# The entry of the odd layer, written out by hand over four engines: x's root before ctx's share, keys and values tile by tile

## The chip, the cores and the metric

The kernel runs on one core of one Trainium2 chip. The metric is the device time of one execution in microseconds; times inside an execution are microseconds from the start of its profiled span. PE is the matmul engine (TensorE), PEld its weight loads, DVE VectorE, ACT ScalarE, POOL GpSimd, and SP the engine whose queue issues most loads.

## The reference

Two layers of a transformer over 512 tokens `x` and 256 context tokens `ctx`, width 1024. Each layer modulates a normalised input, mixes tokens, and adds a gated feed-forward part (FFN). Around the change stand the end of layer 0's FFN and the entry of layer 1 (the odd one):

```python
y = xf * lax.rsqrt(jnp.mean(xf * xf, axis=-1, keepdims=True) + EPS)      # rmsnorm, then * g
modulate(x, g, shift, scale) = rmsnorm(x, g) * (1 + scale) + shift
q, k, v = jnp.split(h @ w_qkv, [C_Q_WIDTH, C_Q_WIDTH + C_KV_WIDTH], axis=-1)   # 1024, 256, 256 columns
q, k = apply_rope(q, cos, sin), apply_rope(k, cos, sin)
kc, vc = jnp.split(hc @ w_qkv[:, C_Q_WIDTH:], 2, axis=-1)                # ctx gives keys and values, no queries
```

The odd layer then attends in blocks of 128 queries, each to a band of three blocks of x's keys and to all of ctx's keys, with a sink in the softmax. ctx itself is not needed after this layer's keys and values.

## The kernel before

Everything lies transposed: eight tiles of 128 features (`m` or `k`, 0 to 7) by 512 columns of x or 256 of ctx. Each float32 factor is split in a high part (a cast on ACT) and a low part (the difference, on POOL or DVE), and `mm3` (L102) multiplies with three matmuls, high by high, high by low and low by high (L106, L107, L108): one product. `unit` (L73) loads 128x512 of a weight over SP into one of a few raw buffers and splits it (L81 ACT, L84 POOL) into a slot of the ring; a load waits until POOL is done with its raw buffer, a split until PE is done with its slot.

PSUM has eight banks: `bank` takes the next of three, `fill` a single one, `single` the next of four, or in their place `wide` the next of two pairs. A tile that is asked for again waits until the last reader of its old contents is done. SBUF pools are stacked from the left and from the right; a tile of a pool opened in the place of a released one waits for the readers of what lay there.

A planner orders the instructions of each engine by its own model of time. Where an instruction is issued under `tc.issue_after(other)`, it stays behind the other one on its engine. `run` (L876) uses that: whatever is issued with `run("PE", ...)` (or "DVE", "ACT", "POOL") forms a chain in the order of the code.

`ffn(0)` works on 22 hidden blocks, in a list of units written as letters (L1084): digits are products of the first FFN matrix, `s` and `t` parts of the second. `s2_part` (L1049) multiplies two hidden blocks (or one) for feature tile m into a bank, and `residual` (L774) adds the result, times a gate, to x or ctx in SBUF. The last two blocks (20 and 21) are the remainder: six of the eight tiles m take block 20 ahead, for x and for ctx (the units `efghij`, L1255), while block 21 is finished; then a loop (L1272) runs the rest, x's eight tiles first, then ctx's, and behind each tile squares it (`square`, L780) and adds the squares. Three or four tiles of squares are added up, the other four are handed to PE as they are.

`modulated` (L793) then forms the root for x, and for ctx: PE sums the squares over partitions against a matrix of ones (L156, L161), DVE takes the inverse root with three Newton steps in tiny instructions (L135 to L139), and writes it on the diagonal of a 128x128 block for each 128 columns (L173), and PE spreads that to all partitions with one matmul against ones (L183). Each tile k is then modulated in three steps: DVE scales it by gain and root (L199), ACT adds the shift and rounds to the high part (L200), DVE makes the low part (L201). This, and all of `odd`, is left to the planner.

`odd` (L1298) opens its PSUM pools and its ring (three raw buffers, four slots), loads the rotation tables, the mask and the sink (L1308 to L1314), and projects keys: `project_k` (L1321) runs eight products of 512 columns for x and eight of 256 for ctx, rotates x's keys (`rope`, L248, DVE and POOL), and stacks high and low parts for attention (`stack_k`, L270). It does this for two halves of the keys, then projects the values (L1337): for each of eight k, six products of 256 columns (four blocks of x, two of ctx) into six half banks. `project_q` (L1353) projects 128 of q's 1024 columns at a time into the one `fill` bank, which DVE reads when it rotates them; two such projections come before the first `attend`, two more before each of the next three.

Of the kernel before, what the change touches and what calls it, by code (L numbers as in the profile page):

```python
# [14 lines left out]
P = 128  # L15
D = 1024
# [5 lines left out]
NF = HID // P  # L22
EPS = 1e-6
ROT = [i ^ 16 for i in range(32)]


class Builder:
# [12 lines left out]
    def load(self, pool, src, shape, name, dtype=F32, eng=None, bufs=1):  # L40
        t = pool.tile(shape, dtype, name=self.uid(name), tag=name, bufs=bufs)
        (eng or self.nc.sync).dma_start(t, src)
        return t

    def bank(self):
        return self.pp.tile([P, 512], F32, name=self.uid("pb"), tag="b", bufs=3)
# [811 lines left out]
    def ffn(self, l):  # L858
# [14 lines left out]
        todo = [(1, j, k) for j in range(6) for k in range(KT)] if both else []  # L873
        tail, tiles, owed = {}, [], []

        def run(key, fn, *args, **kw):  # L876

            with tc.issue_after(tail[key].ins) if key in tail else ExitStack():
                tail[key] = fn(*args, **kw)  # L879
            return tail[key]  # L880

# [166 lines left out]

        def s2_part(fs, m, W, off, n, chain=False):  # L1049
            ps = self.bank()[:, :n]  # L1050
# [7 lines left out]
            run("DVE", self.residual, l, 5, m, off, n, ps)  # L1058

# [178 lines left out]
        for u in units:  # L1238
# [25 lines left out]
        while jobs:  # L1264
            job()
        sq = self.sumsq()
        if both:
            self.A = [self.ax() for _ in range(KT)]
        parts = ((0, TX), (TX, TC)) if both else ((TC, TC), (0, TC))
        q0 = (4, 5)[l]  # L1270
        more, sqs = [], []
        for off, n in parts:  # L1272
            rest = []
            for m in range(KT):
# [4 lines left out]
                if off == parts[0][0]:  # L1279
                    sqs.append(Tp.tile([P, 2 * NH], F32, name=self.uid("sqs"), tag="T", bufs=12))  # L1280
                eng = nc.vector if both and m in (2, 3) else nc.gpsimd
                self.square(sq, m, off, n, rest, q0, sqs[m][:, off:off + n], eng)
            more.append(rest)
        if both:
            for q, (off, n) in zip(more, parts):
                self.modulated(1, sq, off, n, q)
        else:
            self.dg = Tp.tile([P, TX], F32, name="dg")
            rows = [self.final_rows(sq, q, off, n) for q, (off, n) in zip(more, parts)]
            for r, (off, n) in zip(rows, parts):  # L1290
                self.final(r, off, n)
        self.Rf.release()
        ring.release()
        Tp.release()
        if both:
            self.ada_close()

    def odd(self):  # L1298
        tc, nc, a = self.tc, self.nc, self.a
        self.wp.release()  # L1300
        self.open_wide()
        self.open_ring(512, 3, 4)
        X, C = [[[t[:, c] for t in A] for A in self.A] for c in (slice(0, TX), slice(TX, TA))]
        self.hcp.release()
# [5 lines left out]
        mask = Rk.tile([P, 384], F32R, name="mask")  # L1310
        nc.vector.tensor_copy(mask, mraw)
        identr = Rk.tile([P, P], F32R, name="identr")
        nc.vector.tensor_copy(identr, self.ident)
        nsink = self.load(Rk, a["sink"].partition_broadcast(P), [P, 16], "sink")  # L1314
        sink = Rk.tile([P, 16], F32, name="sink2")
        nc.vector.tensor_copy(sink, nsink)
        nc.vector.tensor_scalar(nsink, nsink, -1.0, None, ALU.mult)

        K = []

        def project_k(n):  # L1321
            W = self.blocks(a["k1"][n])
            kf = Rt.tile([P, TA], F32, name=self.uid("kf"), tag="kf", bufs=1)
            ps = self.wide()
            for off, T, A in ((0, TX, X), (TX, TC, C)):
                self.dense(ps[:, off:off + T], W, A)
            self.rope(ps[:, :TX], kf[:, :TX], tabs)
            nc.scalar.copy(kf[:, TX:], ps[:, TX:TA])
            K.extend(self.stack_k(kf, Rk, TA, "k1", 8))

        for n in range(2):
            project_k(n)

        V = []
        bk = [self.bank() for _ in range(3)]
        acc = [b[:, h * TC:(h + 1) * TC] for b in bk for h in range(2)]
        for kq in range(2):  # L1337
            W = self.blocks(a["v1"][kq], step=256)
            for i in range(4):
                k = kq * 4 + i  # L1340
                for tb in range(6):
                    A = [X[k][p][:, tb * P:(tb + 1) * P] if tb < 4 else C[k][p][:, (tb - 4) * P:(tb - 3) * P]
                         for p in range(2)]
                    self.mm3(acc[tb], A, W[i], k == 0 and tb % 2 == 0, k == KT - 1)
        for tb in range(6):
            v = Rk.tile([P, TC], F32, name=f"v1_{tb}")
            (nc.vector.tensor_copy if tb % 2 else nc.scalar.copy)(v, acc[tb])
            V.append(v)
        Rt.release()
        Rs = tc.alloc_tile_pool(name="att1", bufs=1, side="right", reuse_waits="tile")  # L1350
# [9 lines left out]
        def softmax(g, i, rc):  # L1360
# [9 lines left out]
            for x in range(4):  # L1370
# [10 lines left out]
                for b in range(b0, b1):  # L1381
                    if b != i:
                        m0, c = (b - i + 1) * P, st + (b - b0) * P
                        nc.tensor.matmul(ps[:, c:c + P], identr, mask[:, m0:m0 + P], start=False, stop=True,
                                         skip_group_check=True)
# [86 lines left out]
        Rs.release()  # L1472
        Rk.release()
        self.ffn_open(1)
        self.ffn_mod(1, 0)
# [98 lines left out]
```

## Time and profile before

| | |
|---|---|
| three runs | 1588.81, 1589.42, 1590.37 us (median 1589.42) |
| profiled execution | 1588.33 us, its span 1586.3 us |
| granted clock of PE | 0.988 |
| busy: PE, PEld | 1518.7 us (96%), 1352.2 us (85%) |
| busy: DVE, POOL, ACT | 1084.7 us (68%), 830.7 us (52%), 723.3 us (46%) |

The span is the time from the first instruction to the last; the profiled execution's time is 2.0 us longer. A share is busy time over span. A row of the timeline reads: start, duration, engine, line, operation, output<-inputs, shapes, count, and in brackets the idle time of the engine just before, with what ended it. A chain is followed back from the last instruction, at each step to what released it; its shares say which engine the time passed through.

### The profile page before, as it was taken

The numbers are of one execution on the slowest core, as the hardware profiler recorded it, in microseconds if no ns is written. First come the engines' busy times: TensorE is split into PE (matmuls) and PEld (weight loads), VectorE is DVE, ScalarE is ACT, GpSimd is POOL, SyncE is SP. The second block draws the span as 40 slices with busy tenths as digits, with TensorE's granted clock in tenths as the row PEclk, the third lists the DMA queues.
The fourth block names the chain that finished last, engine by engine and source line by source line (L and its number), as shares of the span: only waits on it lengthen the run. The fifth ranks groups of instructions, "written<-read, shape, count | busy, mean of one in ns | idle before, by whom it ended". The sixth has DMA issues, their size and how long they took to land.

```text
span 1586.3 us, 24984 instructions
## 1 busy us (share of the span) xinstructions
PE 1518.7 (96%) x9547; PEld 1352.2 (85%) x9547; DVE 1084.7 (68%) x1958; ACT 723.3 (46%) x1472; POOL 830.7 (52%) x565
## 2 busy tenths in 40 slices
PE   6999988999999999999999989999999999999996
PEld 4776877889989999999999978777869989999996
DVE  4720788765688788888785585765667976666656
ACT  2412676553552333333333244565655644444443
POOL 0463211061256776677676415531304398888883
PEclk9999999999999999999999999999999999999998
DMA  8845100033223333454451012110225132323301
GB/s 328 308 145 188 40 8 1 3 131 133 67 80 113 114 120 106 140 166 147 164 165 57 27 52 80 61 34 14 68 80 206 54 120 88 113 92 109 94 14 54
DMA packets 54295, 162.00 MB, mean 102 GB/s; under 512 B 6176, under 2 KB 10656, under 8 KB 46496
## 3 DMA queue, kind: packets, MB, share of 16 engines
q1 hardware_dynamic: 47120, 135.11, 25.5%
q10 hardware_dynamic: 7056, 25.30, 4.9%
q8 instruction: 75, 1.23, 0.3%
q14 instruction: 44, 0.36, 0.1%
HBM read 158.29 MB, written 2.10 MB: 101 GB/s over the span
## 4 chain that ended last, share of the span: by engine, by line
PE 83%; DVE 10%; ACT 3%; issue 2%; DMA 1%; POOL 0%; POOLq 0%; SPq 0%; DVEq 0%; ACTq 0%
PE pw L106 11%; PE pw L107 11%; PE pw L108 11%; PE pb L107 8%; PE pb L106 8%; PE pb L108 8%; PE pf L106 4%; PE pf L107 4%; PE pf L108 4%; PE pb L1427 2%; PE pb L1416 2%; PE pf L359 2%; PE pw L1379 1%; PE pw L1387 1%; PE pw L542 1%
## 5 line engine op out<-in xcount | busy, mean ns | idle before, releaser
L84 POOL TENSOR_TENSOR w<-raw,w 128x512 fp32r<-128x512 f32 (+1 forms) x84 | 127.5, 1525 | 242.9 <-ACT w L81 220.5
L107 PE MATMUL pw<-ax,w 128*128 128x384 f32 (+2 forms) x732 | 233.9, 320 | 3.7 <-DVE ax L201 2.3
L106 PE MATMUL pw<-ax,w 128*128 128x384 f32 (+2 forms) x732 | 232.9, 322 | 4.1 <-DVE q L879 1.9
L108 PE MATMUL pw<-ax,w 128*128 128x384 f32 (+2 forms) x732 | 233.1, 320 | 0.1
L774 DVE SCALAR_TENSOR_TENSOR xT<-pb,mod,xT 128x512 f32<-128x512 f32 (+3 forms) x208 | 145.7, 707 | 125.8 <-PE pb L108 125.5
L879 POOL TENSOR_TENSOR w<-raw,w 128x512 fp32r<-128x512 f32 x110 | 169.4, 1555 | 19.7 <-ACT w L879 19.5
L879 POOL TENSOR_TENSOR w<-t,w 128x512 fp32r<-128x512 f32 x99 | 148.6, 1504 | 55.6 <-ACT w L879 55.6
L106 PE MATMUL pb<-hh,w 128*128 128x512 f32 x480 | 171.0, 356 | 2.3 <-DVE xT L774 2.3
L108 PE MATMUL pb<-hh,w 128*128 128x512 f32 x480 | 171.5, 357 | 0.3 <-DVE w L879 0.3
L107 PE MATMUL pb<-hh,w 128*128 128x512 f32 x480 | 171.1, 356 | 0.0
L107 PE MATMUL pw<-T,w 128*128 128x384 f32 (+1 forms) x508 | 156.9, 310 | 1.2 <-DVE T L123 1.2
L106 PE MATMUL pw<-T,w 128*128 128x384 f32 (+1 forms) x508 | 156.3, 310 | 1.1 <-DVE hs L879 1.1
L108 PE MATMUL pw<-T,w 128*128 128x384 f32 (+1 forms) x508 | 157.0, 310 | 0.0
L106 PEld LDWEIGHTS pw<-ax,w 128*128 128x128 f32 x732 | 138.5, 190 | 12.5 <-DVE q L879 2.6
L107 PEld LDWEIGHTS pw<-ax,w 128*128 128x128 f32 x732 | 139.0, 190 | 11.2 <-DVE ax L201 3.6
L106 PE MATMUL pf<-ax,w 128*128 128x256 f32 (+2 forms) x420 | 139.9, 333 | 7.9 <-DVE qf L252 5.0
L108 PEld LDWEIGHTS pw<-ax,w 128*128 128x128 f32 x732 | 139.2, 190 | 3.1 <-DVE w L948 0.4
L107 PE MATMUL pf<-ax,w 128*128 128x256 f32 (+2 forms) x420 | 138.8, 330 | 0.0
L108 PE MATMUL pf<-ax,w 128*128 128x256 f32 (+2 forms) x420 | 138.7, 330 | 0.0
L879 POOL TENSOR_TENSOR hh<-hs,hh 128x768 fp32r<-128x768 f32 (+1 forms) x42 | 80.7, 1922 | 90.0 <-ACT hh L879 67.6
L879 POOL TENSOR_TENSOR w<-rawo,w 128x512 fp32r<-128x512 f32 x59 | 103.5, 1754 | 30.1 <-ACT w L879 30.1
L228 DVE SCALAR_TENSOR_TENSOR junk<-ar,cb 128x1024 bf16<-128x1024 f32 x64 | 105.6, 1651 | 0.0
(378 smaller groups left out, 3936.8 us busy)
## 6 DMA issues: line engine op xcount, KB each, us to landing
raw<-ffn_in SPq DMA_DIRECT2D x44, 1024.0 KB, 5.1
ar<-ada SPq DMA_DIRECT2D x24, 1024.0 KB, 6.9
ar<-ada ACTq DMA_DIRECT2D x48, 512.0 KB, 3.5
rawo<-ffn_out SPq DMA_DIRECT2D x88, 256.0 KB, 3.0
raw<-odd_out SPq DMA_DIRECT2D x32, 256.0 KB, 2.7
raw<-qk SPq DMA_DIRECT2D x16, 256.0 KB, 7.9
raw<-uv SPq DMA_DIRECT2D x16, 256.0 KB, 2.7
raw<-even_out SPq DMA_DIRECT2D x8, 512.0 KB, 3.5
```

The costliest lines, as they stand in the source:

```text
L84: eng.tensor_tensor(lo, raw, hi.bitcast(F32), ALU.subtract)
L106: mm(out, s[0], m[0], start=start, stop=False, **kw)
L107: mm(out, s[0], m[1], start=False, stop=False, **kw)
L108: return mm(out, s[1], m[0], start=False, stop=stop, **kw)
L228: return self.nc.vector.scalar_tensor_tensor(junk, t, 1.0, self.cb[who], ALU.mult, ALU.mult, accum_out=self.acc[who][:, col:col + 1])
L359: nc.tensor.matmul(ps[32 * q:32 * q + 32, :w], cst[:, k, :], t[:, w * q:w * q + w], start=k == 0, stop=k == KT - 1, skip_group_check=True)
L542: nc.tensor.matmul(ps[:, :TX], Q[c][:, qs], K[c][p][:, :TX], start=p == 0, stop=p == 1)
L774: ins = self.nc.vector.scalar_tensor_tensor(h, ps[:, r], self.modcol(l, j, m, who), h, ALU.mult, ALU.add)
L879: tail[key] = fn(*args, **kw)
L1379: nc.tensor.matmul(ps[:, st:en], Q, K[g][p][:, b0 * P:b1 * P], start=p == 0, stop=p == 1, skip_group_check=True)
L1416: last = nc.tensor.transpose(pt[:, x * P:(x + 1) * P], es[2 * (x % 2) + x // 2][:, kb * P:(kb + 1) * P], self.ident)
L1427: nc.tensor.matmul(po[64 * h:64 * h + 64, :], V[vb][:, 64 * g:64 * g + 64], t[:, h * TC:h * TC + TC], start=kb == 0, stop=kb == nb - 1, sk ...
```

## The change

The end of layer 0's FFN and the entry of `odd` up to the values become one function, `seam`, in which nearly everything on PE, DVE, ACT and POOL runs in the chains of `run` (now a method whose chains outlive `ffn`).

- Four tiles instead of six take block 20 ahead (`efgh`), and only for x. x's eight tiles come first, then ctx's with both blocks in one accumulation, some of them ahead of and some behind x's root; their residuals and squares are spread over the later steps.
- x's squares are added into three tiles (0+1+2 on POOL, 3+4+5+6 on DVE, 7 alone), ctx's into two. The root takes nine tiny steps instead of ten, and one instruction writes the whole diagonal.
- Eight loads of k's and v's weights (512 columns each) get eight slots of their own and four raw buffers; four are issued at the start of the seam, the other four during x's first modulations. All eight stay for ctx.
- x's tiles are modulated in order, DVE's three steps of a tile together, and after a tile its keys (`K`) and values (`V`) are multiplied, in the order written in the string `order`; `s` is the sum of ctx's squares, `d` the spread of ctx's root. ctx is modulated and multiplied last.
- Rotation and stacking of all keys come behind x's products, ctx's columns separately. Mask, identity and sink are copied after the modulations; of the mask only the two outer blocks are kept.
- `project_q(1)` takes a `bank` instead of the `fill` bank. ctx's memory is released only after the attention.

```diff
-                      ("215s6s3s7sef4ghij", "215s6s3s7sef4g")[l]):
+                      ("215s6s3s7sef4gh", "215s6s3s7sef4g")[l]):
...
-                for off, n in whos:
-                    s2_part((NF - 2,), m, Wl[m][:1], off, n, True)
+                s2_part((NF - 2,), m, Wl[m][:1], 0, TX, True)
...
+    def seam(self, s2_part, Wl, ahead):
+        self.open_ring(512, 3, 4)
+        kept = self.ring, self.ring_cfg
+        self.open_ring(512, 4, 8)
...
+        W = [part(*load(v)) for v in src[:4]]
...
+        def diagonal(ps, T):
...
+            run("DVE", ve.tensor_scalar, v, ps[:, :T].rearrange("p (j f) -> p j f", f=P)[:, :, 0], 1.0 / D, EPS, ALU.mult, ALU.add)
+            run("DVE", ve.tensor_scalar, y.bitcast(I32), v.bitcast(I32), -0.5, float(0x5F1FFFF9), ALU.mult, ALU.add)
...
+            run("DVE", ve.scalar_tensor_tensor, dg.rearrange("p (j f) -> p j f", f=P), y.unsqueeze(2).to_broadcast([P, n, P]),
+                0.375 * ROOT, self.ident.unsqueeze(1).to_broadcast([P, n, P]), ALU.mult, ALU.mult)
+            return dg
...
+        for m in range(KT):
+            k = int(m < ahead)
+            s2_part(fs[k:], m, Wl[m][k:], 0, TX, True)
+            square(0, m)
+            if m in (1, 2):
+                add("POOL", 0, 0, m)
+            elif m > 4:
+                add("DVE", 0, 3, m - 1)
...
+        for m in (0, 1):
+            c_unit(m, self.bank)
+        ps = self.fill()
+        sums(ps, [sq[0, m] for m in (0, 3, 7)], TX)
+        for m in (0, 1):
+            c_residual(m)
+        c_unit(2, self.bank)
+        for m in (3, 4):
+            c_unit(m, self.single)
+        dg = diagonal(ps, TX)
+        rx = spread(dg, self.fill())
+        for m in (5, 6):
+            c_unit(m, self.bank)
+        c_residual(2)
+        c_unit(7, self.bank)
...
+        def mod(who, k, r):
...
+            run("DVE", nc.vector.scalar_tensor_tensor, t, h, s, r, ALU.mult, ALU.mult)
+            run("ACT", nc.scalar.activation, out[0], t, AF.Identity, bias=sh)
+            return lambda: run("DVE", nc.vector.scalar_tensor_tensor, out[1], t, sh, out[0].bitcast(F32), ALU.add, ALU.subtract)
...
+        between = {0: [5], 1: [6], 2: [3], 3: [4], 4: [7]}
+        order = iter("K0 V0 K1 V1 K2 K3 V2 s K4 V3 d K5 V4 K6 V5 K7 V6 V7".split())
...
+        for k in range(KT):
+            rest = mod(0, k, rx)
+            for m in between.get(k, ()):
+                c_residual(m)
+            rest()
+            if k < 4:
+                W.append(part(*load(src[4 + k])))
+            if k == 2:
+                for m in (1, 2, 5):
+                    add("DVE", 1, 0, m)
+            elif k == 3:
+                add("DVE", 1, 0, 6)
+                add("DVE", 1, 0, 3)
+            elif k == 4:
+                add("DVE", 1, 0, 4)
+            if k < 5:
+                products(("V0", "V1", "K2", "V2", "V3")[k])
+            elif k == 6:
+                csum.append(diagonal(csum[0], TC))
+                products("d")
+        rests = []
+        for k in range(KT):
+            rests.append(mod(1, k, csum[2]))
+            if k:
+                rests.pop(0)()
+        rests.pop()()
+        products("V7")
...
+        for n in range(2):
+            self.rope(kps[n], kfs[n][:, :TX], tabs)
+        kc = self.single()
...
+        for k in range(KT):
+            k_c(k)
...
+        for k in range(KT):
+            v_c(k)
...
+        with tc.issue_after(self.tail["DVE"].ins):
+            nc.vector.tensor_copy(mask, mraw.rearrange("p (a c) -> p a c", a=3)[:, 0::2, :])
...
-            ps = self.fill()
+            ps = (self.bank if n == 1 else self.fill)()
```

More of the change, by code (lines that the diff above doesn't have):

```diff
@@ L23 @@
 EPS = 1e-6
+ROOT = 0.703952253
 ROT = [i ^ 16 for i in range(32)]
@@ L1265, in ffn @@
             job()
+        if both:
+            ring.release()
+            Tp.release()
+            self.ada_close()
+            self.seam(s2_part, Wl, ahead)
+            return
         sq = self.sumsq()
[L1267 to L1270, printed above, removed]
+        parts, q0 = ((TC, TC), (0, TC)), 5
         more, sqs = [], []
@@ L1280, in ffn @@
                     sqs.append(Tp.tile([P, 2 * NH], F32, name=self.uid("sqs"), tag="T", bufs=12))
-                eng = nc.vector if both and m in (2, 3) else nc.gpsimd
-                self.square(sq, m, off, n, rest, q0, sqs[m][:, off:off + n], eng)
+                self.square(sq, m, off, n, rest, q0, sqs[m][:, off:off + n], nc.gpsimd)
             more.append(rest)
[L1284 to L1291, printed above, removed]
+        self.dg = Tp.tile([P, TX], F32, name="dg")
+        rows = [self.final_rows(sq, q, off, n) for q, (off, n) in zip(more, parts)]
+        for r, (off, n) in zip(rows, parts):
+            self.final(r, off, n)
         self.Rf.release()
@@ new lines, in seam, with square, add, sums @@
+        sq = {}
+        def square(who, m):
+            T = (TX, TC)[who]
+            sq[who, m] = Qp.tile([P, T], F32, name=self.uid("sq"), tag=f"sq{who}", bufs=8)
+            run("ACT", nc.scalar.activation, sq[who, m], self.h(who, m), AF.Square)
+        def add(key, who, to, m):
+            run(key, {"DVE": nc.vector, "POOL": nc.gpsimd}[key].tensor_tensor, sq[who, to], sq[who, to], sq[who, m], ALU.add)
+        def sums(ps, tiles, T):
+            n = T // P
+            for i, t in enumerate(tiles):
+                for j in range(n):
+                    c = slice(j * P, (j + 1) * P)
+                    run("PE", nc.tensor.matmul, ps[:, c], t[:, c], self.ones, start=i == j == 0, stop=i == len(tiles) - 1,
+                        skip_group_check=True)
@@ new lines, in spread, with c_unit @@
+        def spread(dg, out):
+            run("PE", nc.tensor.matmul, out[:, :dg.shape[-1]], self.ones, dg, start=True, stop=True)
+            return out[:, :dg.shape[-1]]
+        fs = (NF - 2, NF - 1)
+        for m in range(KT):
[6 more added lines that the diff above has]
+                add("DVE", 0, 3, m - 1)
+        cps = {}
+        def c_unit(m, bank):
+            cps[m] = bank()
+            s2_part(fs, m, Wl[m], TX, TC, True, cps[m])
@@ L1317, in odd @@
[L1317 to L1329, printed above, removed]
```

145 lines of the change are left out of this document (111 added, 34 removed).

## The prediction

> **What bounds the kernel now.** I read the page first: the span, the PE row of its slices and the shares of the chain that ended last.
>
> ```profile
> span 1586.3 us, 24984 instructions
> PE   6999988999999999999999989999999999999996
> PE 83%; DVE 10%; ACT 3%; issue 2%; DMA 1%; POOL 0%; POOLq 0%; SPq 0%; DVEq 0%; ACTq 0%
> ```
>
> PE is 83% of the chain and its slices hold nines to the end, so a microsecond taken out of the seam between the layers reaches the end unless the next stage idles more: the slices of the attention (26 to 30, counted from 1) are nines too, and have little slack in which a gain would vanish. Then I cut the seam into stages by windows; the columns after the window are its length, then busy time of PE, PEld, DVE, ACT and POOL, the granted clock and the DMA share.
>
> ```profile
> 904.40:921.60 17.20, 16.49 (x86) 13.81 (x85) 15.36 (x27) 5.20 (x9) 1.30 (x1) 1.00 0.00 0
> 921.60:935.40 13.80, 10.85 (x88) 9.86 (x86) 10.40 (x35) 4.95 (x12) 1.99 (x2) 1.00 0.29 92
> 935.40:945.00 9.60, 7.94 (x21) 5.63 (x22) 9.52 (x17) 5.06 (x8) 4.39 (x3) 0.64 0.26 82
> 945.00:975.80 30.80, 30.07 (x222) 28.59 (x221) 18.18 (x35) 13.60 (x24) 13.49 (x10) 1.00 0.23 69
> 981.40:993.30 11.90, 8.12 (x30) 6.21 (x29) 5.85 (x11) 3.18 (x6) 8.14 (x6) 0.86 0.21 67
> 937.20:944.00 6.80, 5.53 (x14) 3.84 (x13) 6.76 (x13) 3.03 (x5) 3.18 (x3) 0.50 0.37 116
> 985.00:988.40 3.40, 3.40 (x9) 2.62 (x9) 0.00 (x0) 0.00 (x0) 2.42 (x2) 0.50 0.41 145
> ```
>
> PE idles 3.0 us around the root (921.6 to 935.4), 1.7 while x is modulated, and 3.8 behind the first q projection; and twice, right after such gaps, the clock is granted at half. PE's timeline names the waits.
>
> ```profile
> 921.63 1.06 PE L156 MATMUL pf<-ones,sq 128*128 128x128 f32 x8
> 922.52 1.73 PE L161 MATMUL pf<-ones,sqs 128*128 128x128 f32 x14
> ...
> 932.76 1.10 PE L183 MATMUL pf<-q,ones 128*128 128x512 f32 x2 [1.41 <-DVE sm L164]
> 935.45 0.50 PE L106 MATMUL pw<-ax,w 128*128 128x512 f32 x1 [1.60 <-ACT ax L200]
> ...
> 975.83 0.40 PE L106 MATMUL pf<-ax,w 128*128 128x512 f32 x1
> 984.07 0.47 PE L106 MATMUL pf<-ax,w 128*128 128x512 f32 x1 [2.60 <-DVE qf L252]
> 993.37 0.50 PE L106 MATMUL pf<-ax,w 128*128 128x512 f32 x1 [1.24 <-DVE qf L252]
> ```
>
> Eight passes of a sum take 0.89 us (921.63 to 922.52): 0.11 each, eight for a tile of x. The projection of q's first columns (q0) begins at 975.83; the second (q1) waits 2.60 us for the one bank that DVE reads late, and the third (q2) 1.24.
>
> **The change, term by term.** Everything on PE goes by the spacing of matmuls in a full stream; a product is three of them.
>
> ```profile
> 915.48 0.39 PE L106 MATMUL pb<-hh,raw 128*128 128x512 f32 x1
> 916.16 0.39 PE L106 MATMUL pb<-hh,raw 128*128 128x512 f32 x1
> ...
> 962.15 0.28 PE L106 MATMUL pb<-w,ax 128*128 128x256 f32 x1
> 962.51 0.28 PE L106 MATMUL pb<-w,ax 128*128 128x256 f32 x1
> ```
>
> So a product of 512 columns costs 0.68 us, one of 256 costs 0.36. The other engines' durations:
>
> ```profile
> 909.34 1.22 DVE L879 TENSOR_TENSOR hh<-hs,hh 128x384 fp32r<-128x384 f32 x2
> 921.12 0.75 DVE L774 SCALAR_TENSOR_TENSOR xT<-pb,mod,xT 128x512 f32<-128x512 f32 x1
> 926.04 0.95 DVE L791 TENSOR_TENSOR sq<-sq,sqs 128x256 f32<-128x256 f32 x2
> 927.36 0.16 DVE L164 TENSOR_SCALAR sm<-pf 128x4 f32<-128x4 f32 x1 [0.37 <-PE pf L161]
> 930.14 0.17 DVE L137 TENSOR_TENSOR sm<-sm 128x4 f32<-128x4 f32 x1
> 930.34 0.16 DVE L138 SCALAR_TENSOR_TENSOR sm<-sm,sm 128x4 f32<-128x4 f32 x1
> 933.89 1.41 DVE L199 SCALAR_TENSOR_TENSOR t<-xT,mod,pf 128x512 f32<-128x512 f32 x2 [0.23 <-PE pf L183]
> 942.03 0.74 DVE L201 SCALAR_TENSOR_TENSOR ax<-t,mod,ax 128x512 fp32r<-128x512 f32 x1
> 942.80 0.75 DVE L199 SCALAR_TENSOR_TENSOR t<-xT,mod,pf 128x512 f32<-128x512 f32 x1
> ...
> 944.25 0.75 DVE L199 SCALAR_TENSOR_TENSOR t<-xT,mod,pf 128x512 f32<-128x512 f32 x1
> ```
> ```profile
> 920.54 0.63 ACT L787 ACTIVATE sqs<-xT 128x512 f32<-128x512 f32 x1 [0.73 <-DVE xT L774]
> 935.31 1.12 ACT L81 CAST w<-raw 128x512 fp32r<-128x512 f32 x2
> 943.65 0.73 ACT L200 ACTIVATE ax<-t,mod 128x512 fp32r<-128x512 f32 x1 [0.72 <-DVE t L199]
> ```
>
> *First term, up to the first modulation.* Before, DVE starts it at 933.89. After: the last gated tile's low part ends at 910.56 in this trace; two ctx parts ahead of it (0.36 each) go, so 909.8. x's eight parts need 4 x 0.68 + 4 x 1.36 = 8.2 us: 918.0. The last residual (0.75), its square (0.63) and their handovers end at 919.6; two ctx parts (1.4 us) and the sums of the two tiles added up earlier (16 passes, 1.8 us) cover that, and the third tile ends the sums at 922.1. The root is nine small steps, 0.20 apart (930.14 to 930.34), and one 512-wide step that I take as the 0.74 of L201: 924.7. Three ctx parts cover 2.1 us of it. From the spread's start to the first modulation the rows give 1.13 (932.76 to 933.89): 926.0. That is 7.9 us sooner. Two tiles of x's sums and three of ctx's go with it. Four weight casts (1.12 us for two) now stand ahead of x's squares on ACT; x's first four parts hide them, and without that cover the squares would begin 2.3 us late, which the sums would see only in part. POOL subtracts for these four (1.31 each, row below) and adds two squares, some 8 us from 910 on, done when the sums begin at 919.5. The eight loads on SP are the same as before, only issued sooner.
>
> *Second term, until ctx's root.* The new order keeps DVE's three steps of a tile together: scale, wait for ACT, low part, next tile. By the rows: 942.80 to ACT's start at 943.65 is 0.85, ACT 0.73, a handover of 0.05 and 0.66 of L201 before the next can issue (two L199 end after 1.41, so the second issued 0.66 behind the first): about 2.25 us a tile, where the old order overlapped tiles (942.80 to 944.25, 1.45). Before PE's spread of ctx's root stand seven tiles (15.8), six adds of 0.47 (2.8) and the root at 256 columns (nine steps and an add's width, 2.3): 20.9. PE's own work there is 5 x 1.36 + 4 x 1.44 + 0.9 = 13.5 us, so **DVE becomes the bound here** and PE waits some 6 us in all, the longest, about 3 us, ahead of that spread, with the last three key tiles and four value tiles queued behind it in PE's fixed order. POOL's share follows:
>
> ```profile
> 936.15 1.25 DVE L137 TENSOR_TENSOR sm<-sm 128x2 f32<-128x2 f32 x1
> 937.32 0.73 DVE L199 SCALAR_TENSOR_TENSOR t<-xT,mod,pf 128x512 f32<-128x512 f32 x1
> ```
> ```profile
> 935.99 2.62 POOL L84 TENSOR_TENSOR w<-raw,w 128x512 fp32r<-128x512 f32 x2 [4.04 <-ACT w L81]
> ```
>
> A two-column step of 0.16 us took 1.25 because a POOL subtraction (1.31 each) was running: DVE steps whose operands all lie in SBUF wait for it, while L199, which reads PSUM, ran at 0.73 beside POOL. Low parts, adds and root are of the first kind. Four weight subtractions are put between the first tiles; up to four of q's may be placed there too: 0 to 8 x 1.31 = 10.5 us. Most fall into DVE's waits for ACT, as the step order above leaves 0.8 us in each tile; I take 1.5. The spread is then at 926.0 + 22.4 = 948.4.
>
> *Third term, to q0.* PE has left 0.4 for the spread, three key tiles (4.1), four value tiles (5.8), and ctx's keys and values, 32 products of 256 columns (11.5): 21.8 us, nothing of it waiting for weights, which stay loaded in their slots. ctx's keys reuse the bank of x's first keys, read by DVE after ctx's modulations: 0.5. The clock: after a wait of 2.60 us it was at half for 3.4 us, which costs 1.7 of PE; a wait of about 3 us is likely to do it again, 1.4 taken, 0 to 3.4 possible. q0 begins at 948.4 + 23.7 = 972.1, against 975.83: 3.7 us sooner.
>
> The Trainium skill ("TensorE: Matmul & The Clock Gate", Part 1) has the clock fall only after a whole idle window of about 3.4 us. By it this 1.4 would be nothing and the sum 1.4 us lower; the row with 2.60 us and half a clock behind it speaks against that, and decides.
>
> *Fourth term, q1.* It now takes another bank than q0's, so it no longer waits until DVE has rotated q0: 2.60 us, 1.7 of half clock, and q2's 1.24 go (q2's bank was q0's, read long before), 5.5 in all. DVE then meets the stacking of q0 with the rotation of q1, which lay apart before; nothing shows its price; between 0 and the 2.60 that the same engine cost here I take 1.0. Net 4.5.
>
> *At nothing:* mask, identity and sink copies move behind the modulations on DVE, under ctx's products (1 us if uncovered); K's stacking is now all behind x's products, beside 11.5 us of ctx's products and 5.4 of q0 (8 x 0.68), and its first reader comes after q1; uncovered it would cost what it overruns.
>
> *Sum.* 3.7 + 4.5 = 8.2 us. The profiled execution took 1588.33 us (its span and 2.0 around it), so 1580.1; the runs' median is 1.1 above it: **1581.2 us**.
>
> **The rivals.**
>
> ```profile
> SPq L42 <- PE pb L108: 32.3, 1, 32.3
> ```
> ```profile
> raw<-k SPq DMA_DIRECT2D x4, 256.0 KB, 3.5
> ```
>
> *Late weights.* In this trace SP stood 32.3 us in front of the mask's load, whose memory a matmul of the last FFN part still read, with k's loads queued behind. If the second four weight loads land behind cos, sin, mask and sink again, they start after the last ctx part (928.2 by the walk) and some 1.5 us of issues, land 3.5 later, 933.2, and ACT, in order, holds the second tile's activation behind the first of those casts: about 4.5 us on the second term. 1585.7. For it: the old order did just that. Against: they wait for raw buffers alone, free by about 912.
>
> *POOL takes DVE's port (the slower side).* If all eight subtractions meet an SBUF-only step, the second term grows by 10.5 instead of 1.5, and PE's longer waits cost a second half-clock window (1.4 becomes 3.4): 1592.2. It decides against the change once the collisions exceed about 9.7 us, seven of eight. For it is the 1.25 above; against it, that only four subtractions are tied to this stage.
> The Trainium skill ("SBUF — State Buffer", "Who interferes with whom") calls the port shared by both engines an exclusive lock for a whole instruction. The trace agrees: 1.25 us for a 0.16 step.
>
> *Smooth.* No collision, no half clock, no meeting at q1, no bank wait: 1.5 + 1.4 + 1.0 + 0.5 less, 1576.8.
>
> *No effect.* The planner places the attention's instructions anew and loses there what the seam gains: 1589.4. The nines of its slices speak against slack that could swallow it, not against a worse order.
>
> **How the numbers follow.** Forecast 0.56, late weights 0.16, POOL 0.12, smooth 0.10, no effect 0.06. A measurement of this kernel can tell about 0.2%, 3.2 us, from no change. Faster by more: forecast, smooth and three quarters of late weights, 0.78; within: the rest of these and no effect, 0.10; slower: 0.12. The range reaches from the smooth case to past the late weights, 1576.5 to 1588.5, and leaves out no effect and POOL, 0.18.
>
> **What would show it.** The first modulation of x near 926 (sums of three tiles, then one root); L199's successor 2.25 us apart a tile; a PE wait of about 3 us ahead of the second L183-like spread, and a half-clock window behind it; q0 near 972 and q1 right behind it without a wait on DVE. Wrong would be: PE waits on ACT or POOL for weights in the first tiles, SBUF-only DVE steps of over 1 us in the tile loop, or scores that wait for K's stacking after q1.

## The result and the profile after

The changed kernel takes 1590.13 us (median of 14 runs) against 1590.30 for the kernel before (14 runs beside them): a ratio of 1.0004, 95% interval 0.9995 to 1.0013. (Ratios here and below are taken over all runs, not from the two medians; the means of these runs also give 1.0004.) No change can be told; 1581.2 was forecast. The page of after answers the three lines that were shown first of before; its profiled execution took 1590.34 us.

```profile
span 1588.6 us, 24909 instructions
PE   6999988999999999999999989999999999999996
PE 81%; DVE 10%; ACT 4%; issue 2%; POOL 1%; DMA 1%; SPq 0%; POOLq 0%; DVEq 0%; ACTq 0%
```

Averages of 40 us show nothing. Two traces are better laid over each other by an instruction that neither kernel changes: the first product of block 20's gated tile with weights read raw. I call its start the **mark** and give later times as distances from it, because the stretch before it differs by up to 2.5 us from profile to profile. The other end is the last norm of the attention's first half (its last transposes into `pb` from `pt`). In before these stand here, with the attention's first scores between them:

```profile
904.41 0.40 PE L106 MATMUL pb<-hh,raw 128*128 128x512 f32 x1
...
991.27 0.39 PE L1379 MATMUL pw<-kh,qa 128*128 128x256 f32 x1
...
1098.35 0.49 PE L1438 MATMUL pb<-ident,pt 128*128 128x128 f32 x3
```

PE's timeline of after has the mark, the spread of ctx's root, the starts of q0, q1 and q2, the first scores, four waits behind them, and the same last norm; in brackets is the idle time and what ended it.

```profile
904.73 0.40 PE L113 MATMUL pb<-hh,raw 128*128 128x512 f32 x1
...
950.76 0.70 PE L49 MATMUL pw<-q,ones 128*128 128x256 f32 x2 [2.54 <-DVE q L49]
...
974.23 0.40 PE L113 MATMUL pf<-ax,w 128*128 128x512 f32 x1
...
979.69 0.39 PE L113 MATMUL pb<-ax,w 128*128 128x512 f32 x1
...
985.13 0.39 PE L113 MATMUL pf<-ax,w 128*128 128x512 f32 x1
...
990.58 0.28 PE L1564 MATMUL pw<-kh,qa 128*128 128x256 f32 x1
...
992.74 0.39 PE L1564 MATMUL pw<-kh,qa 128*128 128x256 f32 x1 [1.42 <-DVE qa L274]
...
1002.36 0.50 PE L113 MATMUL pf<-ax,w 128*128 128x512 f32 x1 [2.26 <-DVE qf L259]
...
1062.65 0.39 PE L114 MATMUL pf<-ax,w 128*128 128x256 f32 x1 [0.42 <-POOL ax L130]
...
1081.44 0.39 PE L114 MATMUL pf<-ax,w 128*128 128x256 f32 x1 [0.42 <-POOL ax L130]
...
1099.04 0.49 PE L1623 MATMUL pb<-ident,pt 128*128 128x128 f32 x3
```

q1 and q2 follow without a wait. By its own distance from the mark q2 is 8.6 us earlier (985.13 - 904.73 = 80.40; before, 993.37 - 904.41 = 88.96), about the forecast's sum of 8.2. Part of that is order: before runs the first scores ahead of q2, after behind it, and these scores start only 1.0 us sooner (85.85 against 86.86), with q2's 5.45 us done ahead of them. By the last norm the lead is gone: 194.31 against 193.94. Between stand a wait of 1.42 before the second scores of the first block, one of 2.26 before q4, which wants the `fill` bank that DVE still reads for q3, and two of 0.42 where a product of the output projection waits for POOL. Windows show the clock behind two of the waits and the stretch from q0 to the last norm; their columns are those of the table of windows in the prediction.

```profile
952.00:955.40 3.40, 3.40 (x15) 3.12 (x14) 2.99 (x7) 1.51 (x4) 0.00 (x0) 0.51 0.00 0
1003.20:1006.60 3.40, 3.40 (x10) 2.63 (x9) 0.18 (x1) 1.45 (x4) 2.68 (x3) 0.51 0.49 152
974.20:999.20 25.00, 23.58 (x109) 19.34 (x108) 12.40 (x22) 8.92 (x15) 17.00 (x12) 1.00 0.21 64
999.20:1034.20 35.00, 32.55 (x175) 25.40 (x175) 23.39 (x47) 18.30 (x40) 19.37 (x16) 0.95 0.17 55
1034.20:1099.00 64.80, 62.78 (x437) 45.48 (x436) 40.18 (x92) 38.26 (x95) 14.09 (x16) 1.00 0.05 16
```

**Theory 1**: the gain of the seam is real; q1's own bank spends it. q1 to q4 run ahead of what DVE, POOL and ACT must do before scores can follow, PE waits there instead of at q1, and every later projection lies one place too early. (The first half of the attention has eight blocks of scores, each followed by its products with the values, and the eight projections q0 to q7; a place is a gap between blocks.) **Theory 2**: half-clock windows come and go and hide a gain. **Theory 3**: what is lost is lost in the seam itself, at its head (ACT and POOL split q's weights while the last FFN part and x's squares wait) and in DVE's step order. A rival to theory 1 says that the attention goes at the pace of DVE, ACT and POOL whatever PE's order.

### The profile page after: what moved, and what is told of

It reads as the page before. It is cut to its first block, busy times and chain, and to the rows that moved or that the text cites. A ratio compares the mean times of both kernels' runs of the same rounds, so it can differ in the third digit from the quotient of the medians.

```text
span 1588.6 us, 24909 instructions
## 1 busy us (share of the span) xinstructions
PE 1517.6 (96%) x9519; PEld 1351.4 (85%) x9519; DVE 1083.1 (68%) x1955; ACT 725.1 (46%) x1480; POOL 831.6 (52%) x565
## 4 chain that ended last, share of the span: by engine, by line
PE 81%; DVE 10%; ACT 4%; issue 2%; POOL 1%; DMA 1%; SPq 0%; POOLq 0%; DVEq 0%; ACTq 0%
PE pw L113 11%; PE pw L115 11%; PE pw L114 11%; PE pb L114 8%; PE pb L115 8%; PE pb L113 8%; PE pf L113 4%; PE pf L114 4%; PE pf L115 4%; PE pb L1612 2%; PE pb L1601 2%; PE pf L366 2%; PE pw L1564 1%; DVE t L49 1%; PE pw L1572 1%
## 5 line engine op out<-in xcount | busy, mean ns | idle before, releaser
L91 POOL TENSOR_TENSOR w<-raw,w 128x512 fp32r<-128x512 f32 (+1 forms) x76 | 114.7, 1516 | 219.7 <-ACT w L88 197.6
L49 POOL TENSOR_TENSOR w<-raw,w 128x512 fp32r<-128x512 f32 x118 | 179.4, 1535 | 37.1 <-ACT w L49 37.0
L113 PE MATMUL pf<-ax,w 128*128 128x256 f32 (+2 forms) x412 | 136.8, 332 | 5.3 <-ACT f L592 2.8
L114 PE MATMUL pf<-ax,w 128*128 128x256 f32 (+2 forms) x412 | 136.0, 330 | 0.8 <-POOL ax L130 0.8
L115 PE MATMUL pf<-ax,w 128*128 128x256 f32 (+2 forms) x412 | 135.6, 329 | 0.0
```

Source lines behind the costliest of these rows:

```text
L49: self.tail[key] = fn(*args, **kw)
L91: eng.tensor_tensor(lo, raw, hi.bitcast(F32), ALU.subtract)
L113: mm(out, s[0], m[0], start=start, stop=False, **kw)
L114: mm(out, s[0], m[1], start=False, stop=False, **kw)
L115: return mm(out, s[1], m[0], start=False, stop=stop, **kw)
```

## The experiments

Each ran in five rounds beside the kernel before; the ratio is to that one.

| run | median us | before, us | ratio | 95% interval |
|---|---|---|---|---|
| bank_alone | 1595.80 | 1590.10 | 1.0033 | 1.0020 to 1.0047 |
| fill_back | 1586.15 | 1590.10 | 0.9978 | 0.9968 to 0.9987 |
| hold3 | 1597.48 | 1590.10 | 1.0052 | 1.0036 to 1.0068 |
| lag | 1586.46 | 1590.10 | 0.9976 | 0.9965 to 0.9988 |
| chain | 1586.33 | 1590.37 | 0.9972 | 0.9963 to 0.9981 |
| lag_fill | 1584.20 | 1590.37 | 0.9966 | 0.9955 to 0.9977 |
| head_fill | 1585.54 | 1590.37 | 0.9970 | 0.9960 to 0.9980 |
| lag_chain | 1583.18 | 1590.37 | 0.9962 | 0.9950 to 0.9974 |
| bank_chain | 1589.73 | 1589.45 | 0.9997 | 0.9985 to 1.0008 |
| chain_fill | 1586.75 | 1589.45 | 0.9982 | 0.9973 to 0.9990 |
| spread | 1599.82 | 1589.45 | 1.0058 | 1.0046 to 1.0071 |
| lag_head_chain | 1579.86 | 1589.45 | 0.9935 | 0.9923 to 0.9948 |

**bank_alone**: one part of the change, put into the kernel before.

```diff
-            ps = self.fill()
+            ps = (self.bank if n == 1 else self.fill)()
```

> The kernel before, with q1 alone moved to a bank of its own, and nothing else of the change. Prediction's fourth term as it stood: q1 follows q0 without its 2.60 us and the half clock behind it, 4.5 us kept to the end, 1585.8. Theory 1 (the own bank lets the planner put every q projection one place earlier, so the last blocks of the attention's first half have none left beside them, and PE waits there instead): q2 starts some 8 us sooner, the scores of the second block do not, the lead is gone by 90 us after q0, total 1589 to 1591.5. Theory 2 (only half-clock windows come and go): the one window of 3.41 us behind q1 goes, 1.7 us kept, 1588.6.

It is slower than before by 0.33%, 5.2 us: worse than any theory had it. PE's timeline, from the mark on:

```profile
906.35 0.40 PE L106 MATMUL pb<-hh,raw 128*128 128x512 f32 x1
...
994.21 0.28 PE L1379 MATMUL pw<-kh,qa 128*128 128x256 f32 x1
...
1007.37 0.72 PE L106 MATMUL pf<-ax,w 128*128 128x512 f32 x1 [4.28 <-DVE qf L252]
...
1104.12 0.49 PE L1438 MATMUL pb<-ident,pt 128*128 128x128 f32 x3
```

The 2.60 us before q1 are gone, and 4.28 stand before q4, again for the bank that DVE reads late. The last norm is 197.77 behind the mark, 3.8 later than in before. The 4.28 alone don't explain it: q4 itself still starts 3.8 us sooner than in before (101.02 behind the mark against 104.84), but with fewer scores done ahead of it. Late in the half more idle time comes in; the run spread below returns to it.

**fill_back**: the same line undone in the changed kernel.

```diff
-            ps = (self.bank if n == 1 else self.fill)()
+            ps = self.fill()
```

> The changed kernel, with q1 back in the bank of q0 and q2. Prediction's fourth term: 4.5 us slower than the changed kernel, 1594.6. Theory 1: q1 waits 2.6 us again, but the projections lie in the attention as they did before, so the attention takes what it took before and the kernel keeps the seam's own gain at q0 (1.9 to 2.2 us): 1587.5 to 1588.8, faster than the changed kernel. Theory 2: the windows decide, 1590 plus or minus 1.7.

0.22% faster than before, 3.5 us: theory 1's sign and a little more than its size; the forecast's fourth term has the wrong sign. In this profile the last norm is 5.4 us sooner than in before (188.52 against 193.94 behind the mark), more than the runs keep; what lies behind that norm was not followed. PE's timeline and the windows from q0 on:

```profile
905.84 0.40 PE L113 MATMUL pb<-hh,raw 128*128 128x512 f32 x1
...
952.20 0.70 PE L49 MATMUL pw<-q,ones 128*128 128x256 f32 x2 [2.52 <-DVE q L49]
...
974.15 0.40 PE L113 MATMUL pf<-ax,w 128*128 128x512 f32 x1
...
981.33 0.50 PE L113 MATMUL pf<-ax,w 128*128 128x512 f32 x1 [1.55 <-DVE qf L259]
...
1094.36 0.60 PE L1623 MATMUL pb<-ident,pt 128*128 128x128 f32 x4
```
```profile
974.20:999.20 25.00, 21.42 (x99) 17.07 (x99) 14.44 (x26) 9.15 (x16) 14.99 (x12) 1.00 0.20 64
999.20:1034.20 35.00, 34.43 (x199) 26.54 (x197) 22.36 (x45) 19.24 (x41) 17.51 (x15) 1.00 0.16 52
1034.20:1094.40 60.20, 59.67 (x423) 44.99 (x423) 40.07 (x94) 36.75 (x91) 16.21 (x17) 1.00 0.06 19
```

In both profiles 721 matmuls lie in these three windows: after in 124.8 us, fill_back in 120.2. Of the 4.6 us, 1.2 are idle PE (5.89 against 4.68, window length less busy time, summed); 1.7 are the half clock (0.95 over 35 us); 1.7 lie in matmuls that count as busy and that these windows don't part further. The idle time alone would never have told the price of the bank. These are single profiles: the 1.7 us of half clock need not come in every run (see the last section).

**hold3**: keep the bank, hold the projections back.

```diff
-            self.dense(ps, self.blocks(a["q1"][n]), X)
+            self.dense(ps, self.blocks(a["q1"][n]), X, blocks[n - 3] if n >= 3 else None)
...
+            blocks.append(last)
```

Here `last` is the last score matmul of a block, and `dense` issues behind it.

> The changed kernel, with the matmuls of each q projection from q3 on held behind the last score of the block three places earlier (q3 behind the scores of block 0, q4 behind those of block 1, and so on), so that each block of the first half has one projection beside it. Theory 1: the 2.26 us in front of q4 and the half clock behind it go, the blocks at 90 us after q0 have filler again, and of the 8.2 us that q2 starts sooner 4 to 7 are kept: 1583 to 1586. Rival (what DVE, ACT and POOL give the scores sets the attention's pace, whatever order PE has): 1589 to 1591.

A miss: 0.52% slower, past both cases. A row of PE's timeline and a window:

```profile
998.86 0.58 PE L1564 MATMUL pw<-kh,qb 128*128 128x256 f32 x1 [5.34 <-ACT e L1578]
```
```profile
996.20:1006.40 10.20, 5.78 (x23) 5.37 (x24) 3.51 (x8) 4.65 (x9) 0.44 (x1) 0.50 0.08 25
```

The scores that I had thought ready were not: the third ones want a bank that ACT's exponentials must empty, and without q3 beside them PE waits 5.34 us, and from within that wait on the clock is granted at half for 10.2 us. So the first half of theory 1 stands (PE is ahead of the other engines there), and its remedy falls: early projections are also what PE does meanwhile.

**chain**: shorten what the scores wait for, and leave the bank.

```diff
-            self.rope(ps, qf, tabs)
+            self.rope(ps, qf, tabs, nc.vector if n < 3 else None)
...
-        nc.gpsimd.tensor_tensor(sh, sh, tabs[1], ALU.mult)
-        nc.gpsimd.tensor_tensor(out, out, sh, ALU.add)
+        eng.tensor_tensor(sh, sh, tabs[1], ALU.mult)
+        eng.tensor_tensor(out, out, sh, ALU.add)
```

The reason is in POOL's timeline of the changed kernel: the two rotation steps of q1 (L260, L261) stand in one queue with the low parts of weights (L91), and take turns with them.

```profile
986.16 1.79 POOL L260 TENSOR_TENSOR sh<-sh,sin 128x512 f32<-128x512 f32 x1 [0.41 <-DVE sh L258]
987.91 1.75 POOL L91 TENSOR_TENSOR w<-raw,w 128x512 fp32r<-128x512 f32 x1
989.62 1.29 POOL L261 TENSOR_TENSOR qf<-qf,sh 128x512 f32<-128x512 f32 x1
```

> The changed kernel, q1 still in its own bank, with both POOL steps in the rotation of q0, q1 and q2 given to DVE. Theory 1, mended by the runs so far (with its own bank q1 runs ahead of the rotation and stacking of the queries, so PE's wait of 2.60 us only moves to the first scores and to q4, and the projections are one place too early for the rest of the half): with the chain shortened the waits of 1.42 and 2.26 us and the half clock behind them go and the projections lie as before the change; 4 to 5 us less than the changed kernel, 1585 to 1586. Rival (DVE, not POOL, is the end of that chain, so more work on it holds the scores as long): 1589.5 to 1592.

0.28% faster than before, 4.5 us, close to theory 1's 1585 to 1586. PE's two waits are now these; the two of 0.42 late in the half are gone too, since the projections again lie where before had them (q5, q6, q7 and the last norm are each 4.2 us sooner than in before). The edit thus shortens the chain and also moves the projections back by way of the planner; the run does not part the two.

```profile
995.03 0.39 PE L1565 MATMUL pw<-kh,qb 128*128 128x256 f32 x1 [2.27 <-ACT e L1579]
...
1014.56 0.50 PE L113 MATMUL pf<-ax,w 128*128 128x512 f32 x1 [1.05 <-DVE qf L260]
```

**chain_fill and bank_chain**: the same rotation with q1 back in the shared bank, and with its own bank in the kernel before.

> The changed kernel with q1 back in the shared bank and the rotation of q0 to q2 on DVE. Beside the run with its own bank and the same rotation (1586.3) it gives what the bank is worth with the shorter chain. Forecast's fourth term: 1.5 to 4.5 us slower, 1588 to 1591. Theory 1 (PE's work ahead of the first scores is the same, and one wait stands for the other): 1585 to 1587.

> The kernel before, with q1 in its own bank and the rotation of q0 to q2 wholly on DVE; nothing of the seam. If the bank lost only because the queries' rotation and stacking could not follow, the forecast's fourth term holds here: 4.5 us less than before, 1585.5 to 1586.5. If a bank of its own gives nothing whatever the chain (PE's wait only changes its place): 1589 to 1591.

chain_fill is 0.18% faster than before, chain 0.28%; the intervals overlap. With the shared bank the rotation on DVE brings no gain by itself that can be told (fill_back, without it, has 0.22%). bank_chain can't be told from before, ratio 0.9997. With the shorter chain the own bank no longer costs, but it doesn't bring the 4.5 us either: the forecast's fourth term holds in none of these runs. The wait changes its place, as the second case of bank_chain's expectation says. The kernel before with the rotation on DVE and the shared bank was not run.

**spread**: are the blocks late in the half that have no projection beside them a cost of their own? q5, q6 and q7 are held behind products with the values. (By the edit these are block 0's first ones for q5, but the last ones of block 1 and of the third block for q6 and q7, not the first as expected below.)

```diff
-            self.dense(ps, self.blocks(a["q1"][n]), X)
+            self.dense(ps, self.blocks(a["q1"][n]), X, marks[(0, 3, 6)[n - 5]] if n > 4 else None)
```

> The changed kernel, q1 in its own bank, with q5, q6 and q7 held behind the first products with the values of block 0, of block 1, and of the third block, which is about where the kernel before has them; the entry as in the changed kernel. If the blocks without a projection beside them cost the changed kernel some 2 us late in the half: PE's waits from 60 us after q0 on fall from 1.9 to under 0.7 us, and the total to 1587.5 to 1588.5. If blocks lose as much wherever the projections are taken from, or the entry is all: 1589.5 to 1592.

0.58% slower, the worst of all, and past both cases. A PE row and a window show what came in: without q5 the next transposes wait for ACT, and the clock falls.

```profile
1012.84 0.69 PE L1601 MATMUL pb<-ident,e 128*128 128x128 f32 x2 [2.39 <-ACT e L1578]
```
```profile
1012.50:1019.30 6.80, 6.46 (x25) 4.39 (x26) 3.95 (x10) 4.36 (x11) 0.74 (x1) 0.50 0.02 8
```

PE's waits from 60 us after q0 on rose instead of falling (gaps of over 0.2 us sum to 3.5 us there, in the changed kernel to 1.9), so the run doesn't say what the missing late projections cost the changed kernel. What this run shows is that taking them from the early blocks costs more. The other traces say something on the late ones, side by side: these gaps sum to 1.9 us in the three runs whose projections lie one place early to the end (the changed kernel, bank_alone, lag), and to 0.3 or 0.4 in the kernel before and in the runs whose q5 to q7 are spaced as in it (fill_back, chain, chain_fill, bank_chain and the pairs; 0.9 in lag_head_chain). So some 1.6 us of the bank's price is idle time late in the half; whether more is lost there stays open.

**lag**: the seam's own step order. DVE's low part of x's tile k goes behind the scale of tile k+1.

```diff
-            rest = mod(0, k, rx)
+            rests.append(mod(0, k, rx))
...
-            rest()
...
+            if k:
+                rests.pop(0)()
...
-            if k < 5:
-                products(("V0", "V1", "K2", "V2", "V3")[k])
+            if 0 < k < 6:
+                products(("V0", "V1", "K2", "V2", "V3")[k - 1])
```

> The changed kernel, with the low part of x's tile k put behind the scale of tile k+1 on DVE, so that DVE no longer waits for ACT within a tile. Seam: a tile takes 1.5 to 1.7 us on DVE instead of 2.2, ctx's spread comes 3 to 5 us sooner, and q0's end too. Prediction's way of adding terms: all of it is kept, 1585 to 1587. Theory 1: the attention's order is the same as in the changed kernel, so what comes sooner is spent in the same waits, at most 1.5 us kept, 1588.5 to 1590.5.

0.24% faster than before, 3.8 us: theory 1's strong form, that whatever comes sooner is spent in the same waits, falls. PE's timeline has the spread of ctx's root without a wait ahead of it, and one wait at the scores:

```profile
953.08 0.60 PE L49 MATMUL pw<-q,ones 128*128 128x256 f32 x2
...
989.33 0.38 PE L1565 MATMUL pw<-kh,qa 128*128 128x256 f32 x1 [2.28 <-DVE qa L274]
```

The spread is not sooner (48.2 behind the mark at 904.84, after 46.0), against the expectation: the planner now puts 22 of q0's matmuls into the wait that stood ahead of it. The lead shows at q1's start, 70.57 behind the mark against 74.96 in the changed kernel, and is still there at the last norm (189.26 against 194.31), so it is kept, as the prediction's way of adding has it, although the projections lie one place early here too. The gain is real work in place of idle time.

**lag_fill, head_fill, lag_chain**: pairs. head_fill has a new edit; `hold` is the last activation of x's tiles on ACT.

```diff
+            with tc.issue_after(self.hold.ins) if n < 2 else ExitStack():
+                W = self.blocks(a["q1"][n])
```

> The changed kernel with q1 back in the shared bank and x's low parts one tile behind on DVE, the two edits that each gave some 4 us. If the two act at different places (DVE within the seam; the order in the attention): both are kept, 1582 to 1583. If both only fill the same PE wait ahead of the first scores: 1585.5 to 1587.

> The changed kernel with q1 back in the shared bank, and the casts of q0's and q1's weights on ACT held behind the last activation of x's tiles. Theory 3 (at the head of the seam ACT and POOL handle query weights while the first FFN part and x's squares wait, 2.4 us): the first modulation comes 2 to 2.5 us sooner, near 926.4, and the total is 1583.5 to 1584.5. Rival (ACT has room there; the first modulation hangs on PE's own order): within 1 us of the 1586.2 that the shared bank alone gave. A cost of holding them would show as q0 waiting for its weights.

> The changed kernel with its own bank for q1, x's low parts one tile behind on DVE, and the rotation of q0 to q2 wholly on DVE. If the two edits act at different places: 1581 to 1583, the lowest so far. If DVE is then too full between the seam and the first scores: 1585 to 1588, with PE waits of over 2 us ahead of the first scores.

lag_fill is 0.34% faster than before: between its two cases, above either edit alone (0.24% and 0.22%) and below their sum (0.46%), with intervals that overlap those of the single edits; q1 now waits 2.89 us for q0's bank. lag_chain is 0.38% faster and misses its better case by 0.2 us; a wait of 2.61 us ahead of its scores remains. In head_fill the mark is at 905.59 and DVE's timeline has x's first modulation here:

```profile
928.04 0.75 DVE L49 SCALAR_TENSOR_TENSOR t<-xT,mod,pf 128x512 f32<-128x512 f32 x1 [1.32 <-PE pf L49]
```

That is 22.45 behind the mark; fill_back has 24.37. The 1.9 us at the head are as theory 3 has them. Of the total 0.08% more than in fill_back (1.3 us) arrive, within the intervals: the milestone is theory 3's, the total (1585.54) the rival's.

**lag_head_chain**: the three edits together, with q1 in its own bank.

> The changed kernel with its own bank for q1, x's low parts one tile behind on DVE, the rotation of q0 to q2 on DVE, and the casts of q0's and q1's weights held behind the last activation of x's tiles. If the 1.9 us that the held casts gave at the first modulation adds to the others: 1581 to 1582, below both kernels by 0.5%. If PE's waits ahead of the first scores take it: 1583 to 1584.5.

1579.86 us, 0.65% faster than before (interval 0.52 to 0.77%), below the expectation's better case and faster than both kernels. Its PE timeline:

```profile
903.85 0.40 PE L113 MATMUL pb<-hh,raw 128*128 128x512 f32 x1
...
1087.55 0.60 PE L1628 MATMUL pb<-ident,pt 128*128 128x128 f32 x4
```

The last norm is 183.70 behind the mark, 10.2 us sooner than in before, and the total is 10.3 sooner: behind that norm nothing is lost. Beside lag_chain the held casts bring 0.27%, 4.3 us, more than in head_fill; why is open. In the profiles 1.7 us of it are a second half-clock window behind the first scores, which lag_chain has and this run has not. Whether the shared bank would do as well in this version was not tried.

## Why the prediction was wrong

*Fourth term: the step that failed.* "Net 4.5" for q1's bank came from adding up the waits that go. They went, and the term still had the wrong sign. The bank alone cost 5.2 us in the kernel before, and in the changed kernel it costs 4.1 (1.0004 against 0.9978). From 4.5 less to 4.1 or 5.2 more is 8.6 to 9.7 us; the forecast missed by 8.9. I priced DVE's meeting of stackings and rotations at 1.0, bounded by the 2.60 that the wait had cost before. That bound was no bound: behind q1 stood q2, q3 and q4, each of which needs the same DVE, POOL and ACT again, and the planner moved them forward. The price came as waits of 1.42 and 2.26 and a half clock in the changed kernel, as 4.28 in bank_alone, and in both as some 1.6 us of idle time late in the half. That the bank is the cause is shown from both sides (put in alone, taken out alone). That it acts by the rotation and stacking behind it rests on chain and bank_chain, where the price is gone; a part of the price, 1.7 us between fill_back and the changed kernel, is not traced further.

*The rival that came true* is "no effect", at 0.06: the planner places the attention's instructions anew and loses there what the seam gains. I had set the nines of the attention's slices against it. They show that before had little idle time, not that another order would have as little; I said so of the rival and gave it no weight.

*First term.* 21.6 us behind the mark was forecast (926.0 - 904.41), 24.05 came (928.78). The rows at the head show why, on four engines:

```profile
909.53 0.62 ACT L88 CAST w<-raw 128x512 fp32r<-128x512 f32 x1 [3.00 <-DMA raw<-q]
910.05 0.51 ACT L49 CAST hh<-hs 128x384 fp32r<-128x384 f32 x1
910.23 1.27 POOL L91 TENSOR_TENSOR w<-raw,w 128x512 fp32r<-128x512 f32 x1 [0.86 <-ACT w L88]
...
910.59 1.32 DVE L49 TENSOR_TENSOR hh<-hs,hh 128x384 fp32r<-128x384 f32 x1 [0.81 <-ACT hh L49]
910.61 0.49 PE L113 MATMUL pb<-hh,raw 128*128 128x512 f32 x1 [0.85 <-ACT hh L49]
```

ACT waits for the DMA of a q weight and keeps the cast of the last gated tile behind it, and DVE's low part takes 1.32 beside POOL's subtraction. I had counted q's weights on POOL and none on ACT. head_fill, with these casts held, comes to 22.45: 1.6 of the 2.45 us that are missing in the changed kernel (1.9 beside fill_back). Two sums of the prediction are slightly off without consequence: 924.7 and 1.13 make 925.8, not 926.0, and 9.7 us of collisions are over seven subtractions (9.2), not seven.

*Second and third terms: right.* From the first modulation to ctx's spread 22.4 us were forecast and 22.0 came (928.78 to 950.76); from there to q0 23.7 and 23.5, with the wait of 2.54 us and the half clock as described. DVE's period of a tile is 2.2, and the collisions with POOL are there:

```profile
928.78 0.75 DVE L49 SCALAR_TENSOR_TENSOR t<-xT,mod,pf 128x512 f32<-128x512 f32 x1 [1.32 <-PE pf L49]
...
930.99 0.74 DVE L49 SCALAR_TENSOR_TENSOR t<-xT,mod,pf 128x512 f32<-128x512 f32 x1
...
935.39 2.32 DVE L49 TENSOR_TENSOR sq<-sq,sq 128x256 f32<-128x256 f32 x3
```
```profile
935.58 1.38 POOL L49 TENSOR_TENSOR w<-raw,w 128x512 fp32r<-128x512 f32 x1 [0.90 <-ACT w L49]
```

Three adds take 2.32 where 0.47 each was taken: the one that meets POOL's subtraction lasts 1.40 us, the other two 0.42 and 0.43. The three terms together were to bring q0 3.7 us sooner; the changed kernel shows 1.9 from the mark, fill_back, where no half clock followed the spread, 3.1. That fill_back's total (3.5 us less than before) comes so near to 3.7 is in part luck: its first term falls short as well (24.37), and its last norm was 5.4 us sooner.

*Late weights* did not happen: PE has no wait of 0.35 us or more for a weight in the seam. *POOL takes DVE's port* happened in part, at the head and in the adds (the prediction's sign of being wrong, an SBUF-only step of over 1 us in the tile loop, came with the 1.40), without deciding.

## What to carry to other kernels

A wait for a buffer is not worth its length until you know what the released engine does next: give the buffer alone in an experiment before adding its wait to a sum. Where a planner orders the work, the matmuls that need nothing are the filler of the waits to come: in this kernel the bank, which moved them forward, cost 4 to 5 us, and holding them back (hold3, spread) another 7.6 and 8.6. Lay traces over each other at an unchanged instruction, and follow a gain milestone by milestone until it vanishes: the step at which it vanishes names the experiment.

## What the runs showed of the hardware that was not expected

The same wait brings a half-clock window or not. 2.54 us ahead of ctx's spread in the changed kernel had one (the window 952.00 to 955.40 above, 0.51); 2.52 at the same place in fill_back had none:

```profile
952.20:955.60 3.40, 3.40 (x21) 3.08 (x22) 2.42 (x5) 1.55 (x3) 0.00 (x0) 1.00 0.02 5
```

What differs is where the wait falls. In all fourteen traces the granted clock changes only at points of a grid with steps of 3.41 us, and the grid's place against the program differs from trace to trace. In the changed kernel 2.17 us of the wait lie in one step, the one ahead of the half clock; in fill_back a grid point (950.40) cuts the wait into 0.72 and 1.80:

```profile
948.59:952.00 3.41, 1.24 (x6) 1.05 (x7) 2.46 (x12) 0.60 (x1) 0.00 (x0) 1.00 0.02 5
```
```profile
950.40:953.81 3.41, 1.61 (x7) 1.38 (x8) 2.38 (x10) 0.72 (x1) 0.00 (x0) 1.00 0.02 5
```

Over the fourteen traces, each of the 66 steps at full clock with more than 1.91 us of idle PE is followed by a step at half clock, none of the 6136 steps with less than 1.5 us is, and in between both occur. So a wait of 2 to 3 us may or may not bring a half clock, by where it falls on the grid, and one of under 1.5 us brought none unless other idle time fell into the same step.

2.26 us ahead of q4 were enough, against the whole idle window of about 3.4 us that the Trainium skill ("TensorE: Matmul & The Clock Gate", Part 1) asks for; these rows decide. A window costs 1.7 us of PE, so a single profile can differ by that much from another of the same kernel: theory 2 explains such differences, but not the signs above, which the runs' intervals hold.
